# Moving the value transposes between weight pieces, and the last products with values into the scores' PSUM banks

## The chip, the cores and the metric

The kernel runs on one core of a Trainium2 chip, as one launch. The metric is the device time of the execution in microseconds. Before the change three runs gave 1260.53, 1256.4 and 1260.03 us, median 1260.03.

## What is computed

One layer of a streaming encoder, for 256 prompt frames and 64 frames of a running stream: 320 columns in all (T), held transposed, with features on the partitions. Weights and activations are float32.

```
z = rmsnorm(x) @ w_in                 # 2048 -> 1024 q | 128 k | 128 v | 1024 u | 1024 gate
q, k = rmsnorm(q), rmsnorm(k)         # per head of 64; 16 query heads, 2 kv heads
w = softmax(q k / 8 + bias, sinks)    # chunks of 64, own chunk and the two before
a = w @ v
s = gelu(u) * (W_s rmsnorm(gelu(g)) + b)
x = x + [rmsnorm(a), rmsnorm(s)] @ w_out
y = x + relu(rmsnorm(x) @ w_up)^2 @ w_down
```

Outputs are y, the new keys and values, and the normalised gate rows of the stream's frames.

## The kernel before, in words

**Products by weight pieces.** Every large product computes 256 output features for all 320 columns (`product`, `products`, L115 to L153). It goes through the contraction in pieces of four 128-row tiles. For each piece one DMA loads 128x1024 weights (`w_raw`), ScalarE rounds them to the high half `w_hi` (L108), VectorE subtracts to get the low half `w_lo` (L109), and TensorE runs 24 matmuls of 128x320 (L134): for each of four tiles and two output halves the high weights with the high and the low activations, and the low weights with the high ones. There are three slots each of `w_hi` and `w_lo`. A product with 2048 input features has four pieces, 0 to 3.

**Small work between pieces.** `between_pieces` names functions that run behind a piece: its instructions are issued after the last matmul of that piece, and the matmuls of the pieces behind it are issued after the last matmul on the list `narrow` (variable `behind`), the latest of the small TensorE instructions. When the function stands behind a product's last piece, `carry` takes that mark to the next product; otherwise it ends with the product (L141). A scheduler in the framework fills in the rest of each engine's order.

**PSUM.** `acc` has two slots of two banks for the products; `s_ps` one slot of two banks (`ps_sc`, used first for the product q0, later for attention scores); `misc` two slots of one bank each, for everything small.

**The stretch that is changed.** The products of the input projection run in this order: keys, values and q0 together, q1, q2, q3, then four for the gate (v), then four for u.

- Behind piece 2 of q2, `keys` normalises the keys, sends them and the values to the outputs, copies them to the shape that the scores need (two DMAs from GpSimd's queue, L353 and L354), and calls `values`: five TensorE transposes of 96 or 128 value columns (L326), each into a `misc` slot, each copied by VectorE to `vz` (L328).
- Behind q2, VectorE evicts its sums to `qT` (L303, `evict_q`) and ScalarE squares them (`qsq`, L308).
- Behind piece 1 of q3, `norm_q(2)` sums these squares with five small matmuls (L314, ten rows of the trace) and `attend(0)` computes the first scores (L392).
- The attention has ten units (five blocks of queries by two kv heads). `attend(i)` runs three stages: `values_of(i-3)` multiplies the turned probabilities with the values (L447) into a `misc` slot, which ScalarE copies to `ao` (L450); `scores(i)` fills `s_ps`, and VectorE, ScalarE and GpSimd make probabilities of it (L402 to L421); `turn(i-2)` transposes these (L435) in one or two parts of four transposes, each part into a `misc` slot that VectorE copies out (L437). There is one `attend` behind each of pieces 1 and 3 of q3 and the v products; `attend(10)` and `attend(11)` stand behind pieces 1 and 3 of the first u product, `attend(12)` behind piece 1 of the second. From `attend(10)` on there are no scores left. `attend(11)` is followed by `rstd_rows` (L159), whose three sums take a `misc` slot too.

Of the kernel before, what the change touches and what calls it, by code (L numbers as in the profile page):

```python
# [8 lines left out]
F32 = mybir.dt.float32  # L9
# [6 lines left out]
P = 128  # L16
# [14 lines left out]
def hymba_step_kernel(ctx: ExitStack, tc: tile.TileContext, i, o):  # L31
    nc = tc.nc
# [9 lines left out]
    ps_sc = ctx.enter_context(tc.tile_pool(name="ps_sc", bufs=1, space=bass.MemoryType.PSUM))  # L42
    ps_m = ctx.enter_context(tc.tile_pool(name="ps_m", bufs=2, space=bass.MemoryType.PSUM))

    def misc():
        return ps_m.tile([P, 512], F32, name="misc", tag="misc")
# [68 lines left out]
    def products(w, k0, nk, c0, ps, rh, rl, deep=None, between_pieces={}, halves_behind={}):  # L115

        wv = w.rearrange("(kt p) n -> p kt n", p=P)
        behind = carry.pop() if carry else None  # L120
        steps.clear()
        for a in range(0, nk, 4):
            raw = (deep or wp).tile([P, 4, 256], F32, name="w_raw", tag="w_raw")
            hi, lo = w_tiles()
            load(raw, wv[:, k0 + a:k0 + a + 4, c0:c0 + 256])
            with tc.issue_after(halves_behind[a // 4]()) if a // 4 in halves_behind else nullcontext():
                high, low = halves(raw, hi, lo)
            tail = isinstance(ps, list) and a + 4 == nk
            for k, g in [(k, g) for g in range(2) for k in range(4)] if tail else [(k, g) for k in range(4) for g in range(2)]:
                kk = a + k  # L130
                for x, (w_, r_) in enumerate(((hi, rh), (hi, rl), (lo, rh))):
                    out = ps[g][:, 0:T] if isinstance(ps, list) else ps[:, g, 0:T]
                    with tc.issue_after(behind) if behind else nullcontext():
                        mm = nc.tensor.matmul(out=out, lhsT=w_[:, k, g * P:(g + 1) * P], rhs=r_(kk),  # L134
                                              start=(kk == 0 and x == 0), stop=(kk == nk - 1 and x == 2))
            steps.append((high, low, mm.ins))
            if a // 4 in between_pieces:
                with tc.issue_after(mm.ins):
                    between_pieces[a // 4]()
                    behind = narrow[-1]  # L140
                if a + 4 == nk:  # L141
                    carry.append(behind)
# [4 lines left out]
    def acc_tile():  # L147
        return ps_acc.tile([P, 2, 512], F32, name="acc", tag="acc")

    def product(w, k0, nk, c0, rh, rl, deep=None, apart=False, **kw):  # L150
        ps = [misc(), misc()] if apart else acc_tile()
        products(w, k0, nk, c0, ps, rh, rl, deep=deep, **kw)
        return ps  # L153
# [108 lines left out]
    vz = kzv[:, 896:1664].rearrange("p (x h d) -> p x h d", x=6, h=2)  # L262
    cv = i["cv"].rearrange("k (h d) -> k h d", h=2)
# [37 lines left out]
    def evict_q(g, q_ps):  # L301
        qg = qT[:, :, 2 * g:2 * g + 2]
        nc.vector.tensor_tensor(out=qg.rearrange("p b a t -> p a b t"),  # L303
                                in0=q_ps[:, :, 0:T].rearrange("p a (b t) -> p a b t", b=5),
                                in1=rx.rearrange("p (b t) -> p b t", b=5)[:, None].to_broadcast([P, 2, 5, 64]),
                                op=ALU.mult)
        sq = sm.tile([P, 5, 2, 64], F32, name="qsq", tag="w2", bufs=4)
        nc.scalar.activation(out=sq, in_=qg, func=AF.Square)  # L308
        return sq

    def norm_q(g, sq):
        st = misc()
        for b in range(5):
            mm = nc.tensor.matmul(out=st[:, 2 * b:2 * b + 2], lhsT=sq[:, b].rearrange("p a t -> p (a t)"), rhs=hone,  # L314
                                  start=True, stop=True)
        narrow.append(mm.ins)
        r = at.tile([P, 10], F32, name="r_q", tag="r_q")
        nc.vector.tensor_scalar(out=r, in0=st[:, 0:10], scalar1=HD * EPS, scalar2=None, op0=ALU.add)
        nc.gpsimd.tensor_tensor(out=rq[:, g], in0=r, in1=nhalf[:, 0:10], op=ALU.pow)

    vn = {}

    def values():
        for x, (t0, n) in enumerate(((0, 128), (96, 96), (64, 96), (160, 96), (224, 96))):
            vps = misc()
            narrow.append(nc.tensor.transpose(out=vps[0:n, 0:P], in_=vT[:, t0:t0 + n], identity=ident).ins)  # L326
            vn[t0] = vz[:, x]
            nc.vector.tensor_copy(out=vn[t0][0:n], in_=vps[0:n, 0:P].rearrange("k (h d) -> k h d", h=2))  # L328


# [9 lines left out]
    q1_sq = []  # L340
# [6 lines left out]
    def keys():  # L347
        for dst, c in ((kn[:, 0:256], slice(0, 256)), (kn[:, 384:448], slice(256, 320))):
            nc.vector.scalar_tensor_tensor(out=dst, in0=zk[:, c], scalar=g_k, in1=rk[:, c], op0=ALU.mult, op1=ALU.mult)
        for h in range(2):  # L350
            hs = slice(h * HD, (h + 1) * HD)
            nc.vector.tensor_scalar(out=kz[hs, h], in0=kn[hs], scalar1=g_q[hs], scalar2=None, op0=ALU.mult)
        nc.gpsimd.dma_start(out=kz[HD:P, 0], in_=kz[0:HD, 0])  # L353
        nc.gpsimd.dma_start(out=kz[0:HD, 1], in_=kz[HD:P, 1])  # L354
        nc.gpsimd.dma_start(out=o["kpT"], in_=kn[:, 128:256])
        nc.gpsimd.dma_start(out=o["ksT"], in_=kn[:, 384:448])
        nc.gpsimd.dma_start(out=o["vpT"], in_=vT[:, 128:256])
        nc.gpsimd.dma_start(out=o["vsT"], in_=vT[:, 256:320])
        values()

    q2_ps = product(w_in, 0, KT, 512, xh, xl,
                    between_pieces={0: first_norms, 1: lambda: norm_q(1, q1_sq[0]), 2: keys})
    nc.gpsimd.dma_start(out=vn[224][0:32], in_=cv[96:P])
    q2_sq = evict_q(2, q2_ps)


# [74 lines left out]
    def values_of(u):  # L441
        blk_, kv = units[u]
        q0, parts = blocks[blk_][0], turned.pop(u)
        o_ps = misc()
        for x, (pt, v, n) in enumerate(parts):
            for p in range(2):
                mm = nc.tensor.matmul(out=o_ps[p * HD:(p + 1) * HD, 0:256], lhsT=v[0:n, kv],  # L447
                                      rhs=pt[0:n, p * 256:(p + 1) * 256], start=(x == 0), stop=(x == len(parts) - 1))
        narrow.append(mm.ins)
        nc.scalar.activation(out=ao[:, 4 * kv:4 * kv + 4, q0:q0 + 64],  # L450
                             in_=o_ps[:, 0:256].rearrange("p (a q) -> p a q", a=4), func=AF.Copy)

    def attend(i):

        for stage, u in ((values_of, i - 3), (scores, i), (turn, i - 2)):
            if 0 <= u < 10:
                with tc.issue_after(narrow[-1]):
                    stage(u)

    q3_ps = product(w_in, 0, KT, 768, xh, xl,  # L460
                    between_pieces={1: lambda: (norm_q(2, q2_sq), attend(0)), 3: lambda: attend(1)})
    q3_sq = evict_q(3, q3_ps)

    def add_square(acc, src, first):
# [227 lines left out]
```

## Time and profile before

| | |
|---|---|
| three runs, us | 1260.53, 1256.4, 1260.03 (median 1260.03) |
| profiled execution, us | 1259.32 |
| its span, first to last instruction, us | 1256.6 |
| mean granted TensorE clock | 0.998 |
| TensorE busy | 1246.9 us, 99% of the span |
| VectorE, ScalarE, GpSimd busy | 52%, 39%, 8% |
| memory traffic | 187.78 MB, mean 149 GB/s |

A TensorE row of the timeline gives the start, the duration of the group, line, operation and tiles, and in brackets how long the engine stood idle before it and what released it. Matmuls are pipelined, so a row of 0.31 us starts every 0.15 us. A row of the chain of waits gives start, length, engine, tile, line and count. The view by stretches gives for each engine its busy time, and behind them the granted clock, the DMA share and GB/s.

### The profile page before, as it was taken

The numbers are of one execution on the slowest core, as the hardware profiler recorded it, in microseconds if no ns is written. First come the engines' busy times: TensorE is split into PE (matmuls) and PEld (weight loads), VectorE is DVE, ScalarE is ACT, GpSimd is POOL, SyncE is SP. The second block draws the span as 40 slices with busy tenths as digits, with TensorE's granted clock in tenths as the row PEclk, the third lists the DMA queues.
The fourth block names the chain that finished last, engine by engine and source line by source line (L and its number), as shares of the span: only waits on it lengthen the run. The fifth ranks groups of instructions, "written<-read, shape, count | busy, mean of one in ns | idle before, by whom it ended". The sixth has DMA issues, their size and how long they took to land.

```text
span 1256.6 us, 20213 instructions
## 1 busy us (share of the span) xinstructions
PE 1246.9 (99%) x8519; PEld 1234.4 (98%) x8519; DVE 650.7 (52%) x767; ACT 489.6 (39%) x638; POOL 100.5 (8%) x97
## 2 busy tenths in 40 slices
PE   9999999999999999999999999999999999999998
PEld 8999989999999999999999999999999999999998
DVE  7857765776874544444444444454444334444443
ACT  7335556434543433333333322243333333343221
POOL 1114543300310000000000000000000000000000
PEclk9999999999999999999999999999999999999999
DMA  8644333644454444444454444555444454444550
GB/s 269 209 128 118 110 110 106 204 149 140 150 151 151 150 151 151 151 152 151 150 148 152 147 149 147 150 150 151 151 151 152 150 151 148 147 152 159 169 169 32
DMA packets 186556, 187.78 MB, mean 149 GB/s; under 512 B 6593, under 2 KB 185985, under 8 KB 186465
## 3 DMA queue, kind: packets, MB, share of 16 engines
q1 hardware_dynamic: 185824, 185.43, 47.6%
q8 instruction: 66, 1.08, 0.4%
q0 software_dynamic: 496, 1.03, 0.3%
q14 instruction: 26, 0.20, 0.0%
q10 hardware_dynamic: 144, 0.03, 0.0%
HBM read 182.91 MB, written 3.32 MB: 148 GB/s over the span
## 4 chain that ended last, share of the span: by engine, by line
PE 98%; ACT 1%; DVE 1%; POOL 0%; DMA 0%; issue 0%; SPq 0%; DVEq 0%; POOLq 0%
PE acc L134 91%; PE acc L240 1%; PE q_ps L240 1%; PE misc L134 1%; PE s_ps L392 1%; PE misc L435 0%; PE misc L447 0%; ACT w_hi L108 0%; PE misc L314 0%; DMA w_first<-in_w_in 0%; PE misc L521 0%; PE misc L507 0%; POOL gv L496 0%; POOL gc L479 0%; ACT s L417 0%
## 5 line engine op out<-in xcount | busy, mean ns | idle before, releaser
L109 DVE TENSOR_TENSOR w_lo<-w_raw,w_hi 128x1024 fp32r<-128x1024 f32 x332 | 413.3, 1245 | 438.4 <-ACT w_hi L108 428.7
L108 ACT ACTIVATE w_hi<-w_raw 128x1024 fp32r<-128x1024 f32 x332 | 351.7, 1060 | 705.9 <-PE acc L134 671.3
L134 PE MATMUL acc<-H2H,w_hi 128*128 128x320 f32 x1024 | 316.4, 309 | 0.0
L134 PE MATMUL acc<-H2L,w_hi 128*128 128x320 f32 x1024 | 316.4, 309 | 0.0
L134 PE MATMUL acc<-H2H,w_lo 128*128 128x320 f32 x1024 | 316.4, 309 | 0.0
L134 PE MATMUL acc<-FH,w_hi 128*128 128x320 f32 x992 | 306.5, 309 | 0.0
L134 PE MATMUL acc<-FL,w_hi 128*128 128x320 f32 x992 | 306.5, 309 | 0.0
L134 PE MATMUL acc<-FH,w_lo 128*128 128x320 f32 x992 | 306.5, 309 | 0.0
L134 PEld LDWEIGHTS acc<-H2H,w_lo 128*128 128x128 f32 x1024 | 192.2, 188 | 0.0
L134 PEld LDWEIGHTS acc<-H2H,w_hi 128*128 128x128 f32 x1024 | 192.2, 188 | 0.0
L134 PEld LDWEIGHTS acc<-H2L,w_hi 128*128 128x128 f32 x1024 | 192.2, 188 | 0.0
L134 PEld LDWEIGHTS acc<-FH,w_hi 128*128 128x128 f32 x992 | 186.2, 188 | 0.0
L134 PEld LDWEIGHTS acc<-FL,w_hi 128*128 128x128 f32 x992 | 186.2, 188 | 0.0
L134 PEld LDWEIGHTS acc<-FH,w_lo 128*128 128x128 f32 x992 | 186.2, 188 | 0.0
L134 PE MATMUL acc<-XH,w_hi 128*128 128x320 f32 x352 | 111.5, 317 | 0.0
L134 PE MATMUL acc<-XL,w_hi 128*128 128x320 f32 x352 | 109.3, 310 | 0.0
L134 PE MATMUL acc<-XH,w_lo 128*128 128x320 f32 x352 | 108.8, 310 | 0.0
L134 PEld LDWEIGHTS acc<-XH,w_hi 128*128 128x128 f32 x352 | 66.6, 189 | 0.3
L134 PEld LDWEIGHTS acc<-XL,w_hi 128*128 128x128 f32 x352 | 66.6, 189 | 0.0
L134 PEld LDWEIGHTS acc<-XH,w_lo 128*128 128x128 f32 x352 | 66.4, 189 | 0.0
L609 DVE SCALAR_TENSOR_TENSOR tf<-acc,r 128x640 f32<-128x640 f32 x32 | 26.4, 825 | 41.9 <-PE acc L134 41.8
L623 DVE TENSOR_TENSOR xT<-xT,acc 128x640 f32<-128x640 f32 x31 | 25.5, 821 | 41.8 <-PE acc L134 41.8
(201 smaller groups left out, 1056.6 us busy)
## 6 DMA issues: line engine op xcount, KB each, us to landing
w_raw<-in_w_up SPq DMA_DIRECT2D x128, 512.0 KB
w_raw<-in_w_down SPq DMA_DIRECT2D x128, 512.0 KB
w_raw<-in_w_in SPq DMA_DIRECT2D x44, 512.0 KB
w_raw<-in_w_out SPq DMA_DIRECT2D x32, 512.0 KB
w_first<-in_w_in SPq DMA_DIRECT2D x15, 256.0 KB
out_yT<-xT SPq DMA_DIRECT2D x7, 320.0 KB
xT<-in_xT SPq DMA_DIRECT2D x8, 160.0 KB
xT<-in_xT SPq DMA_DIRECT2D x4, 320.0 KB
```

Source lines behind the costliest of these rows:

```text
L108: return (pin(nc.scalar.activation(out=hi, in_=raw, func=AF.Copy)).ins, pin(nc.vector.tensor_tensor(out=lo, in0=raw, in1=hi.bitcast(F32), ...
L109: pin(nc.vector.tensor_tensor(out=lo, in0=raw, in1=hi.bitcast(F32), op=ALU.subtract)).ins)
L134: mm = nc.tensor.matmul(out=out, lhsT=w_[:, k, g * P:(g + 1) * P], rhs=r_(kk), start=(kk == 0 and x == 0), stop=(kk == nk - 1 and x == 2))
L240: mm = nc.tensor.matmul(out=ps[:, g, 0:T], lhsT=w_[:, j, k, g * P:(g + 1) * P], rhs=r_(a + k), start=(a + k == 0 and x == 0), stop=(a + k ...
L392: mm = nc.tensor.matmul(out=s_ps[:, p, j * nk:(j + 1) * nk], lhsT=qT[hs, blk_, a:a + 2].rearrange("p a t -> p (a t)"), rhs=kz[hs, kv, k0:k ...
L609: nc.vector.scalar_tensor_tensor(out=t, in0=ps[:, :, 0:T], scalar=0.0, in1=r2[:, None, :].to_broadcast([P, 2, T]), op0=ALU.max, op1=ALU.mult)
L623: nc.vector.tensor_tensor(out=xT[:, a:a + n], in0=xT[:, a:a + n], in1=p, op=ALU.add)
```

## The change

`values` takes the indices of the transposes that it is to do. The first two stay behind piece 2 of q2, the next two go behind its piece 3 (the last of the product, so that the mark is carried to q3), and the fifth goes behind piece 0 of q3, with the small DMA that fills the other rows of the same tile. `values_of` takes an `s_ps` slot for units 7, 8 and 9, and a `misc` slot for the others as before.

```diff
-    vn = {}
-
-    def values():
-        for x, (t0, n) in enumerate(((0, 128), (96, 96), (64, 96), (160, 96), (224, 96))):
+    vn = {t0: vz[:, x] for x, t0 in enumerate((0, 96, 64, 160, 224))}
+
+    def values(*xs):
+        for x in xs:
+            t0, n = ((0, 128), (96, 96), (64, 96), (160, 96), (224, 96))[x]
             vps = misc()
             narrow.append(nc.tensor.transpose(out=vps[0:n, 0:P], in_=vT[:, t0:t0 + n], identity=ident).ins)
-            vn[t0] = vz[:, x]
             nc.vector.tensor_copy(out=vn[t0][0:n], in_=vps[0:n, 0:P].rearrange("k (h d) -> k h d", h=2))
...
-        values()
+        values(0, 1)
 
     q2_ps = product(w_in, 0, KT, 512, xh, xl,
-                    between_pieces={0: first_norms, 1: lambda: norm_q(1, q1_sq[0]), 2: keys})
-    nc.gpsimd.dma_start(out=vn[224][0:32], in_=cv[96:P])
+                    between_pieces={0: first_norms, 1: lambda: norm_q(1, q1_sq[0]), 2: keys,
+                                    3: lambda: values(2, 3)})
     q2_sq = evict_q(2, q2_ps)
...
-        o_ps = misc()
+
+        o_ps = ps_sc.tile([P, 2, 512], F32, name="o_ps", tag="s_ps")[:, 0] if u > 6 else misc()
...
+    def last_values_part():
+        values(4)
+        nc.gpsimd.dma_start(out=vn[224][0:32], in_=cv[96:P])
+
     q3_ps = product(w_in, 0, KT, 768, xh, xl,
-                    between_pieces={1: lambda: (norm_q(2, q2_sq), attend(0)), 3: lambda: attend(1)})
+                    between_pieces={0: last_values_part, 1: lambda: (norm_q(2, q2_sq), attend(0)), 3: lambda: attend(1)})
```

Three places in the order of the engines' instructions show what moves. In the names, acc_636 is the sum of q2; acc_828 before, and acc_824 after, is the sum of q3.

TensorE before, just ahead of `norm_q(2)` (L314) and the first scores (L392), with the end of q2's last piece (weights 794 and 795) and of q3's piece 1 (weights 860 and 861):

```order
L134 MATMUL acc_636<-XH_117,w_hi_794 128x320
L134 MATMUL acc_636<-XL_118,w_hi_794 128x320
L134 MATMUL acc_636<-XH_117,w_lo_795 128x320
L134 MATMUL acc_828<-XH_117,w_lo_861 128x320
L134 MATMUL acc_828<-XH_117,w_hi_860 128x320
L134 MATMUL acc_828<-XL_118,w_hi_860 128x320
L134 MATMUL acc_828<-XH_117,w_lo_861 128x320
L314 MATMUL misc_889<-hone_113,qsq_825 128x2 x5
L392 MATMUL s_ps_898<-kzv_438,qT_119 128x64 x4
```

TensorE with the change, some 48 matmuls earlier in the program: the end of q2's last piece (weights 785 and 786), the third and fourth value transposes, and the start of q3:

```order
L134 MATMUL acc_636<-XH_117,w_hi_785 128x320
L134 MATMUL acc_636<-XL_118,w_hi_785 128x320
L134 MATMUL acc_636<-XH_117,w_lo_786 128x320
L327 MATMUL misc_814<-ident_88,kvx_436 96x128
L327 MATMUL misc_817<-ident_88,kvx_436 96x128
L134 MATMUL acc_824<-XH_117,w_hi_826 128x320
L134 MATMUL acc_824<-XL_118,w_hi_826 128x320
```

Before, q2's last matmul stood four matmuls ahead of `norm_q(2)`, behind 44 matmuls of q3; now all of q3's pieces 0 and 1, 48 matmuls, stand between the two.

VectorE before, from the copies of the third and fourth value transposes to `norm_q(2)`'s own step (L318), with the eviction of q2 (L303):

```order
L328 COPY kzv_438<-misc_784 96x128
L328 COPY kzv_438<-misc_787 96x128
L109 TENSOR_TENSOR w_lo_927<-w_raw_925,w_hi_926 128x1024
L328 COPY kzv_438<-misc_790 96x128
L303 TENSOR_TENSOR qT_119<-acc_636,rx_471 128x2x5x64
L109 TENSOR_TENSOR w_lo_957<-w_raw_955,w_hi_956 128x1024
L109 TENSOR_TENSOR w_lo_1020<-w_raw_1018,w_hi_1019 128x1024
L318 TENSOR_SCALAR r_q_895<-misc_889 128x10
```

VectorE with the change, the same stretch:

```order
L303 TENSOR_TENSOR qT_119<-acc_636,rx_471 128x2x5x64
L328 COPY kzv_438<-misc_814 96x128
L328 COPY kzv_438<-misc_817 96x128
L109 TENSOR_TENSOR w_lo_927<-w_raw_925,w_hi_926 128x1024
L328 COPY kzv_438<-misc_855 96x128
L109 TENSOR_TENSOR w_lo_957<-w_raw_955,w_hi_956 128x1024
L318 TENSOR_SCALAR r_q_895<-misc_889 128x10
L109 TENSOR_TENSOR w_lo_1020<-w_raw_1018,w_hi_1019 128x1024
```

The eviction of q2 moved ahead of three copies and a weight piece, and one weight piece moved behind L318.

ScalarE before, from the rounding of q3's piece 1 (w_hi_860) to the squares of q2:

```order
L108 ACTIVATE w_hi_860<-w_raw_859 128x1024
L108 ACTIVATE w_hi_926<-w_raw_925 128x1024
L108 ACTIVATE w_hi_956<-w_raw_955 128x1024
L108 ACTIVATE w_hi_1019<-w_raw_1018 128x1024
L308 ACTIVATE qsq_825<-qT_119 128x640
```

ScalarE with the change:

```order
L108 ACTIVATE w_hi_860<-w_raw_859 128x1024
L108 ACTIVATE w_hi_926<-w_raw_925 128x1024
L308 ACTIVATE qsq_821<-qT_119 128x640
L108 ACTIVATE w_hi_956<-w_raw_955 128x1024
L108 ACTIVATE w_hi_1019<-w_raw_1018 128x1024
```

The squares of q2 moved ahead of the rounding of two weight pieces (the last of q3 and the first of the v products).

In the last three units TensorE's instructions keep their places; the products with values (L447, now L448) write `o_ps` instead of `misc`. On VectorE the second copy of `turn(8)` (L437, to vnat) now stands ahead of a weight piece's L109 that it followed.

## The prediction

> **What bounds the kernel now.** I read the page first, then TensorE's own list of waits, then the chain of waits and the timelines around the two long ones.
>
> The page, span and busy time of the engines:
>
> ```profile
> span 1256.6 us, 20213 instructions
> PE 1246.9 (99%) x8519; PEld 1234.4 (98%) x8519; DVE 650.7 (52%) x767; ACT 489.6 (39%) x638; POOL 100.5 (8%) x97
> ```
>
> TensorE, busy for 99% of the span, sets the time; the change takes no matmul away. It can only win back what TensorE waits or runs slowly, and every microsecond won there moves the end by one. The list of what TensorE's matmuls waited for (total, times, longest):
>
> ```profile
> PE misc L435 <- DVE kzv L437: 2.1, 1, 2.1
> PE misc L314 <- ACT qsq L308: 2.0, 1, 2.0
> PE misc L435 <- ACT ao L450: 0.4, 1, 0.4
> PE misc L159 <- DVE kzv L437: 0.3, 1, 0.3
> ```
>
> All four stand in stretches that the change touches: the second in `norm_q(2)`, the others in `attend(10)`, `attend(11)` and the sums behind it. The chain of waits around the second:
>
> ```profile
> 70.70 3.54 PE acc L134 x24
> 74.26 0.84 DVE qT L303
> 75.10 1.02 ACT w_hi L108
> 76.12 0.64 ACT qsq L308
> 76.80 1.28 PE misc L314 x10
> 78.07 1.03 PE s_ps L392 x8
> 79.10 8.33 PE acc L134 x48
> ...
> 88.07 7.23 PE acc L134 x48
> 95.31 1.01 PE misc L314 x10
> ...
> 124.57 0.59 PE s_ps L392 x8
> ```
>
> TensorE finishes q2 only at 74.2, VectorE then evicts it (L303), ScalarE squares it behind other work, and `norm_q(2)` stands until 76.8. The same work also runs slower than its like elsewhere: 1.28 against 1.01, 1.03 against 0.59 (scores of the same 64 columns), 8.33 against 7.23 for 48 matmuls. The view by stretches shows why, in the column behind POOL, the granted clock:
>
> ```profile
> 78.00:81.50 3.50, 3.50 (x18) 3.38 (x18) 1.84 (x9) 0.61 (x4) 1.98 (x1) 0.51 0.87 280
> ```
>
> In the 3.5 us behind the wait the clock is 0.51.
>
> **The transposes: eviction of q2 comes early.** ScalarE, TensorE and VectorE there:
>
> ```profile
> 67.55 1.06 ACT L108 ACTIVATE w_hi<-w_raw 128x1024 fp32r<-128x1024 f32 x1 [2.90 <-PE acc L134]
> 74.11 2.00 ACT L108 ACTIVATE w_hi<-w_raw 128x1024 fp32r<-128x1024 f32 x2 [5.50 <-PE acc L134]
> 76.02 0.72 ACT L308 ACTIVATE qsq<-qT 128x640 f32<-128x640 f32 x1
> ...
> 76.80 1.28 PE L314 MATMUL misc<-hone,qsq 128*128 128x2 f32 x10 [1.99 <-ACT qsq L308]
> ...
> 63.85 0.49 DVE L328 COPY kzv<-misc 128x128 f32<-128x128 f32 x2 [0.43 <-PE misc L326]
> 65.98 0.93 DVE L352 TENSOR_SCALAR kzv<-kvx,cols 64x448 f32<-64x448 f32 x2
> 74.26 0.82 DVE L303 TENSOR_TENSOR qT<-acc,rx 128x640 f32<-128x640 f32 x1 [3.23 <-PE acc L134]
> ```
>
> All five transposes stand behind piece 2 of q2 and borrow two slots, so the scheduler spread them over the next matmuls; q2's own last piece must follow the fifth, and q3's first 44 matmuls went ahead of it. With the change q2's last piece follows the second transpose directly. The order says so for all three engines. Piece by piece at the trace's pace (24 matmuls 3.54 us): q2 ends about 67.5, where the trace had the end of q3's piece 0; VectorE is free from 66.9 (L352) and evicts 67.6 to 68.4; ScalarE, done with one weight piece at 68.6, squares until 69.3. `norm_q(2)` is reached at about 74.8, where the idle time began (76.80 - 1.99). That leaves 5.5 us of cover, so I take the wait as gone:
>
> - the wait itself: 1.99
> - `norm_q(2)`: 1.28 - 1.01 = 0.27
> - scores: 1.03 - 0.59 = 0.44
> - the 48 matmuls: 8.33 - 7.23 = 1.10
>
> Sum 3.80, of which 1.81 is the slow clock and 1.99 the wait. Without the wait the small work is 1.01 + 0.59 = 1.60 us. Behind piece 1 of the first v product it is longer, 2.37 us with `norm_q(3)`, wider scores and transposes, and the clock stays at 1.00:
>
> ```profile
> 95.14:97.51 2.37, 2.37 (x24) 2.13 (x23) 1.16 (x2) 1.06 (x1) 1.78 (x2) 1.00 0.76 220
> ```
>
> [...]
>
> **What could be late next there.** Transposes three and four now stand ahead of all of q3, at 67.5; their slots must be free, which needs VectorE's first two copies (done 64.34): cover 3.1 us. The fifth at about 71.2 needs a slot from a copy that now stands behind the eviction, about 68.7: cover 2.5. If a cover went, TensorE would stand, since the order has nothing else there. VectorE's weight piece that moved behind L318 (w_lo_1020) is done about 77.1 and needed by the first v product, some 48 matmuls (7.2 us) behind the scores: cover 6. Scores now start at about 75.8 instead of 78.07, and need the two key copies:
>
> ```profile
> 67.26 0.52 POOL L354 DMA_DIRECT2D kzv<-kzv  x1
> kzv<-kzv POOLq DMA_DIRECT2D x2, 112.0 KB, 4.4
> ```
>
> Issued by 67.8 and landed 4.4 later, 72.2: cover 3.6. The cv DMA (L363, now L463) keeps its place in GpSimd's queue, waits for the fifth copy as before, and its rows are read first by `values_of(4)`, in `attend(7)`. I count these at nothing; less than nothing is excluded, since none is waited for now.
>
> **The last three units.** TensorE's rows of the unbroken turn at 162.83 and of `attend(10)`, VectorE's of `attend(11)`, and ScalarE's copy in `attend(10)`:
>
> ```profile
> 162.83 1.08 PE L435 MATMUL misc<-ident,s 128*96 128x128 f32 x8
> 171.89 0.64 PE L435 MATMUL misc<-ident,s 128*96 128x128 f32 x4
> 174.67 0.64 PE L435 MATMUL misc<-ident,s 128*96 128x128 f32 x4 [2.14 <-DVE kzv L437]
> ...
> 183.33 1.22 DVE L109 TENSOR_TENSOR w_lo<-w_raw,w_hi 128x1024 fp32r<-128x1024 f32 x1
> 184.47 0.68 DVE L437 COPY kzv<-misc 96x512 f32<-96x512 f32 x1
> ...
> 174.28 0.36 ACT L450 ACTIVATE ao<-misc 128x256 f32<-128x256 f32 x1
> ```
>
> In `attend(10)` three things want two slots: `values_of(7)`, and the two parts of `turn(8)`. The second part waits 2.14 us for VectorE's copy of the first; ScalarE's copy of the values ends with it at 174.64. With the values in `s_ps`, both parts have a slot at once. Saved: the wait 2.14, and 0.64 + 0.64 - 1.08 = 0.20 of the broken row: 2.34. No dip follows this wait, as 47 matmuls then take 6.91 us, so none is won:
>
> ```profile
> 175.31 6.91 PE acc L134 x47
> ```
>
> `s_ps` is free there: its last reader is VectorE's step on unit 9's scores, which come right ahead of the row of 162.83. It is one slot, so `values_of(8)`, due 2.3 us sooner at about 180, waits for ScalarE's copy of unit 7, done 174.64: cover 5.3.
>
> In `attend(11)` the 0.4 behind ScalarE's copy goes, but the sums (L159, 0.3 in the list) still wait for VectorE's copy of the first part (184.47), which stands behind a weight piece (183.33) that follows TensorE's own pace. I count nothing; at most 0.4 + 0.3 = 0.7. In `attend(12)` I also count nothing.
>
> **Sum.** 3.80 + 2.34 = 6.14 us. The profiled execution took 1259.32, 2.7 of it outside its span of 1256.6 and untouched: 1259.32 - 6.14 = 1253.2. It lies 0.7 below the median of the three runs, inside their spread of 4.1.
>
> **The rivals.**
>
> *A, the dip stays.* The wait goes, and the clock dips all the same, as the small work of 1.60 us is still there. Price 1.81: 1253.2 + 1.8 = 1255.0. For it: a wait as long, 2.14 us, at 174 is followed by no dip, so length alone does not make one. Against it: 2.37 us of small work at 95.14 make none either. [...]
>
> *B, the wait of `attend(10)` moves on.* The second part of `turn(8)` no longer waits, but VectorE's copies stay where they are (that of the first part ended just ahead of 174.67), and something else stands for them. Price 2.34: 1255.5. Against it: no small work that needs a slot follows for two pieces of 3.5 us.
>
> *C, q2's end is early and `norm_q(2)` still waits,* for the scores' keys or a slot, or the order does not hold on the chip: only the second place gains, 1259.32 - 2.34 = 1257.0. Against it: the covers of 3.6 and 5.5.
>
> *D, slower.* The transposes become a gate. Three and four hold all of q3, the fifth holds its piece 1, and TensorE stands for VectorE's copies, with nothing queued that may pass. It decides from a lateness of 3.1 us beyond the trace's pace at the first, 2.5 at the second. To turn the sum, the two waits with a dip of 1.81 each must exceed 6.14, so 2.5 us of waiting in all; to be slower by more than 0.3% (3.8 us) 6.3, or 3.15 each: 1253.2 + 6.3 + 3.6 = 1263.1, with the 0.7 to the median 1263.8. Against it: VectorE, 52% busy over the span, sat idle for 3.23 us ahead of 74.26.
>
> **How the numbers follow.** Forecast 0.66, A 0.11, B 0.10, C 0.06, D 0.03, no change at all 0.04. The likeliest is the forecast, 1253.2. Down, the range takes in the 0.7 of `attend(11)` and the 2.9 by which the fastest of the three runs lies below the profiled one, most of it: 1250.0. Up, it takes in A and B and the 0.7 to the median, 1256.2, and most of C: 1256.6. About 0.3% of the time, 3.8 us, is what a measurement can tell from no change. Faster by more, below 1256.25: forecast, nearly all of A and B: 0.81. Within: C, no change, and the rest: 0.15. Slower: 0.04.
>
> **What would show it.** In the profile of the changed kernel: the eviction of q2 (L303) at about 67.6 and its squares below 70; `norm_q(2)` at about 74.7 with no idle time ahead of it, and the granted clock at 1.00 between 74 and 82 (A if not); the next scores' 48 matmuls in 7.2 us; `turn(8)` in one row of eight at about 168; the last matmul some 6 us earlier in the span. It would be wrong if TensorE's list of waits names L327, L392 or L448 with more than 1 us, or if a wait of 2 us stands at L159.

## The result

| | before | after |
|---|---|---|
| median, us (five runs of each) | 1260.53 | 1251.18 |
| lowest to highest, us | 1256.4 to 1263.5 | 1251.05 to 1252.61 |
| profiled execution, us | 1259.32 | 1251.18 |
| its span, us | 1256.6 | 1249.4 |
| mean granted TensorE clock | 0.998 | 1.000 |

The ratio of after to before is 0.993, 95% interval 0.9908 to 0.9952: faster by 9.35 us at the median, where 6.14 was forecast against the profiled execution. The time lies in the range and 2.0 below the number. One of the twelve executions of e9 below ran at a mean clock of 0.203 and took 5707.55 us; it is left out of e9's row.

The busy times on the page and TensorE's list of waits after the change:

```profile
PE 1243.7 (100%) x8519; PEld 1231.9 (99%) x8519; DVE 650.8 (52%) x767; ACT 489.4 (39%) x638; POOL 102.1 (8%) x97
```

```profile
PE misc L78 <- DVE hone L91: 1.3, 1, 1.3
PE misc L159 <- DVE kzv L437: 0.8, 1, 0.8
```

The wait for the squares (L314) and both waits at L435 are gone. L78 is at the program's start, before as after; L159 has 0.8 where 0.4 (L435) and 0.3 (L159) stood at two places. The chain of waits after, at both places:

```profile
62.79 0.22 PE misc L327 x2
...
73.90 1.01 PE misc L314 x10
74.91 0.59 PE s_ps L392 x8
75.50 7.23 PE acc L134 x48
82.73 0.65 PE s_ps L392 x8
...
167.26 1.01 PE misc L435 x8
168.27 6.90 PE acc L134 x47
...
178.16 0.83 PE misc L159 x6
...
188.02 1.00 PE misc L512 x8
```

All the small work runs at its undisturbed length, and nothing stands between 62.79 and 82.73 but TensorE's own work. The timeline (VectorE's eviction of q2, ScalarE's squares) and the view by stretches, in which the 1.00 behind POOL is the granted clock:

```profile
66.56 0.82 DVE L303 TENSOR_TENSOR qT<-acc,rx 128x640 f32<-128x640 f32 x1 [0.57 <-PE acc L134]
67.42 0.74 ACT L308 ACTIVATE qsq<-qT 128x640 f32<-128x640 f32 x1
```

```profile
78.00:81.50 3.50, 3.50 (x26) 3.50 (x25) 1.36 (x4) 2.48 (x10) 0.83 (x2) 1.00 0.41 139
```

The squares end at 68.16, 5.7 us ahead of their reader at 73.90.

### The profile page after: what moved, and what is told of

Read it like the earlier page. It is cut to its first block, busy times and chain, and to the rows that moved or that the text cites. A ratio compares the mean times of both kernels' runs of the same rounds, so it can differ in the third digit from the quotient of the medians.

```text
span 1249.4 us, 20216 instructions
## 1 busy us (share of the span) xinstructions
PE 1243.7 (100%) x8519; PEld 1231.9 (99%) x8519; DVE 650.8 (52%) x767; ACT 489.4 (39%) x638; POOL 102.1 (8%) x97
## 3 DMA queue, kind: packets, MB, share of 16 engines
q0 software_dynamic: 496, 1.03, 0.3%
## 4 chain that ended last, share of the span: by engine, by line
PE 97%; DMA 2%; SPq 1%; ACT 0%; DVE 0%; issue 0%; ACTq 0%; DVEq 0%
PE acc L134 91%; PE misc L134 1%; DMA w_raw<-in_w_in 1%; SPq L103 1%; PE misc L435 1%; PE s_ps L392 1%; DMA b_dram<-b_row 1%; PE q_ps L240 0%; PE acc L240 0%; PE misc L448 0%; PE misc L314 0%; PE misc L526 0%; PE misc L512 0%; DMA cols<-in_cols 0%; ACT w_hi L108 0%
## 5 line engine op out<-in xcount | busy, mean ns | idle before, releaser
L109 DVE TENSOR_TENSOR w_lo<-w_raw,w_hi 128x1024 fp32r<-128x1024 f32 x332 | 413.7, 1246 | 434.6 <-ACT w_hi L108 425.1
L134 PE MATMUL acc<-H2H,w_hi 128*128 128x320 f32 x1024 | 316.4, 309 | 0.0
L134 PE MATMUL acc<-H2L,w_hi 128*128 128x320 f32 x1024 | 316.4, 309 | 0.0
L134 PE MATMUL acc<-H2H,w_lo 128*128 128x320 f32 x1024 | 316.4, 309 | 0.0
L134 PE MATMUL acc<-FH,w_hi 128*128 128x320 f32 x992 | 306.5, 309 | 0.0
L134 PE MATMUL acc<-FL,w_hi 128*128 128x320 f32 x992 | 306.5, 309 | 0.0
L134 PE MATMUL acc<-FH,w_lo 128*128 128x320 f32 x992 | 306.5, 309 | 0.0
L134 PEld LDWEIGHTS acc<-H2L,w_hi 128*128 128x128 f32 x1024 | 192.3, 188 | 0.0
L134 PEld LDWEIGHTS acc<-H2H,w_hi 128*128 128x128 f32 x1024 | 192.3, 188 | 0.0
L134 PEld LDWEIGHTS acc<-H2H,w_lo 128*128 128x128 f32 x1024 | 192.3, 188 | 0.0
L134 PEld LDWEIGHTS acc<-FH,w_hi 128*128 128x128 f32 x992 | 186.2, 188 | 0.0
L134 PEld LDWEIGHTS acc<-FL,w_hi 128*128 128x128 f32 x992 | 186.2, 188 | 0.0
L134 PEld LDWEIGHTS acc<-FH,w_lo 128*128 128x128 f32 x992 | 186.2, 188 | 0.0
L134 PE MATMUL acc<-XH,w_hi 128*128 128x320 f32 x352 | 111.1, 316 | 0.1
L134 PE MATMUL acc<-XL,w_hi 128*128 128x320 f32 x352 | 108.7, 309 | 0.0
L134 PE MATMUL acc<-XH,w_lo 128*128 128x320 f32 x352 | 108.6, 309 | 0.0
L134 PEld LDWEIGHTS acc<-XH,w_hi 128*128 128x128 f32 x352 | 66.2, 188 | 0.6 <-ACT ksq L338 0.4
L134 PEld LDWEIGHTS acc<-XL,w_hi 128*128 128x128 f32 x352 | 66.2, 188 | 0.0
L134 PEld LDWEIGHTS acc<-XH,w_lo 128*128 128x128 f32 x352 | 66.0, 188 | 0.0
```

The lines of the kernel that those rows point to most:

```text
L109: pin(nc.vector.tensor_tensor(out=lo, in0=raw, in1=hi.bitcast(F32), op=ALU.subtract)).ins)
```

## The experiments

The theory after the result had two parts: each half of the change removes one wait of about 2 us, and a wait can bring a slow stretch of the clock behind it whose cost differs from execution to execution. The rival: the gain beyond 6.1 was luck of single executions, or the slow stretch has another cause than the wait. All medians below stand beside runs of the kernel before on the same chip (medians 1260.5 to 1261.5; e1, e2, e3 and e7 stand beside 1261.5, all others beside 1260.5 to 1260.7). The last column is the mean granted clock, averaged over the runs of the row. With about half of a stretch at half clock taken as lost (1.54 of 3.41 us in e2 below), a mean clock that is 0.001 lower stands, as an estimate, for 1.26 us lost of a span of 1259 us; what is said below of slow clock in medians is this estimate. The runs of before beside them have 0.9961 to 0.9967.

| kernel | median, us (lowest to highest, runs) | ratio to before, 95% | clock |
|---|---|---|---|
| e0, after again | 1251.30 (1250.83 to 1252.79, 5) | 0.9926 [0.9912, 0.9940] | 0.9998 |
| e1, after without the `s_ps` slots | 1256.21 (1255.45 to 1258.21, 6) | 0.9957 [0.9942, 0.9971] | 0.9987 |
| e2, before with the `s_ps` slots | 1256.90 (1256.11 to 1258.68, 6) | 0.9961 [0.9946, 0.9975] | 0.9983 |
| e3, after, squares late | 1256.80 (1253.74 to 1258.19, 6) | 0.9957 [0.9941, 0.9973] | 0.9988 |
| e5, before, squares earlier | 1258.61 (1256.95 to 1262.46, 12) | 0.9985 [0.9975, 0.9996] | 0.9978 |
| e6, after, sums in `s_ps` too | 1250.61 (1250.17 to 1251.59, 4) | 0.9919 [0.9904, 0.9934] | 1.0000 |
| e7, after, squares later still | 1260.23 (1259.09 to 1264.36, 12) | 0.9996 [0.9984, 1.0008] | 0.9962 |
| e8, before, norm_q(2) later | 1254.61 (1253.91 to 1259.17, 9) | 0.9958 [0.9944, 0.9971] | 0.9990 |
| e9, before, wait filled | 1258.25 (1256.52 to 1262.54, 11) | 0.9984 [0.9971, 0.9997] | 0.9988 |
| e11, after, more small work | 1256.03 (1254.31 to 1259.86, 12) | 0.9966 [0.9954, 0.9978] | 0.9985 |

e4 and e10 were one execution each, and their times stand with them.

**Is the gain that large (e0)?** The changed kernel unaltered.

> The changed kernel itself, beside runs of the kernel before on the same chip. By the theory (two waits of 2.0 and 2.1 us gone, and with them whatever slow clock they bring), 1251 to 1253 us again with a mean clock of 1.00 in each run, and 8 to 10 us below the median of before. If the 8.1 us between the two profiled executions were mostly luck of the one execution (0.9 at the start and 0.9 outside the span), about 6.

It is: 1251.30, 9.4 below before. Its profiled span was 1250.2; the 9 us are no luck. The clocks say how much of it is slow clock: 0.9998 against 0.9967 in the 23 runs of before beside it is 3.9 us of a span of 1259.

**Each half alone (e1, e2).**

```diff
# e1, on the changed kernel
-        o_ps = ps_sc.tile([P, 2, 512], F32, name="o_ps", tag="s_ps")[:, 0] if u > 6 else misc()
+        o_ps = misc()
# e2, on the kernel before: the reverse
```

> The change with the products with values back in misc slots. Theory (two separate terms): the wait of norm_q(2) and the slow clock behind it go, 3.8 us of 1260.5, so about 1256.7; TensorE's list keeps about 2.1 us at L435 and has nothing at L314; the 48 matmuls behind the first scores take 7.2 us. Rival (the two places share the misc slots, so one alone brings little): less than 1.5 us is won. Rival (most of the gain is the second place): about 1258.

> The kernel before with only units 7, 8 and 9 in the scores' banks. Theory: turn(8) is one row of eight, 2.3 us are won, about 1258.2; norm_q(2) still waits 2.0 us, and the granted clock of the runs is below 1.00 in those whose dip comes. [...]

e1 gained 5.3 us, e2 4.6: together 9.9, about what both give. The chain of e1, in which L435 waits as before:

```profile
77.17 1.01 PE misc L314 x10
...
78.78 7.23 PE acc L134 x48
...
173.90 6.90 PE acc L134 x47
```

And that of e2:

```profile
77.05 1.28 PE misc L314 x10
...
78.91 8.77 PE acc L134 x48
```

Each half mends its own place only: the first place is clean in e1 (1.01 and 7.23) and still slow in e2, where the slow stretch came later, past the scores (from 80.12), and cost 8.77 - 7.23 = 1.54. The row of `norm_q(2)` has its 1.28 there ahead of the slow stretch: the 0.27 above 1.01 belongs to the wait and not to the clock. The second half was worth more than its 2.34 of wait and broken row: 4.6. The mean clock gives most of the rest: 0.9983 in e2 against 0.9961 is 2.8 us, and e10 shows where it lay in one execution.

**The kernel before once more (e10).** Unaltered, one execution.

> The kernel before once more, for a second profile of it. Its executions on this chip have a mean clock of 0.994 to 0.998. Theory: both waits, 2.0 us near 75 and 2.1 us near 172, can bring a slow stretch, now one and now both, and a run with 0.995 or 0.996 shows a dip behind each, or one of two windows of 3.4 us. Rival: the slow stretches lie elsewhere, away from both waits.

1264.65 us, mean clock 0.994: slower than all 13 runs of before beside it (1257.09 to 1262.95), so a slow example and not a typical one. TensorE's waits and the chain of this execution:

```profile
PE acc L134 <- ACT ksq L338: 2.5, 1, 2.5
PE misc L435 <- DVE kzv L437: 2.1, 1, 2.1
PE misc L314 <- ACT qsq L308: 2.0, 1, 2.0
```

```profile
51.81 5.29 PE acc L134 x24
...
79.75 1.53 PE misc L314 x10
81.28 1.05 PE s_ps L392 x8
82.34 9.56 PE acc L134 x48
...
179.78 8.43 PE acc L134 x47
```

The same two waits, 2.1 and 2.0, but the clock took more: 0.25 (1.53 less 1.28) + 0.46 + 2.33 = 3.0 at the first place and 8.43 - 6.90 = 1.5 at the second, where the execution of the prediction lost nothing. Together 4.6, against 1.54 in the execution of the prediction. A third place is ahead of the change, 2.5 us of waiting near 50 us and 5.29 for 24 matmuls; the wait is in kernels with and without the change (0.5 to 2.5 in most profiles, none in some), a slow stretch follows it in two profiles of fourteen (e10 without the change, e1 with its first half), and it is no part of the change. The view by stretches, cut at the edges of the slow stretches:

```profile
77.19:80.60 3.41, 1.42 (x12) 1.16 (x11) 3.18 (x3) 2.51 (x3) 0.00 (x0) 1.00 0.03 3
80.60:84.01 3.41, 3.41 (x18) 3.28 (x19) 1.69 (x9) 0.00 (x0) 1.98 (x1) 0.50 0.93 290
84.01:87.42 3.41, 3.41 (x14) 3.41 (x14) 0.49 (x4) 1.53 (x9) 0.61 (x1) 0.50 0.06 21
...
176.17:179.58 3.41, 1.28 (x13) 0.86 (x9) 2.14 (x5) 3.27 (x11) 2.54 (x4) 1.00 0.47 147
179.58:182.99 3.41, 3.41 (x15) 3.41 (x14) 1.28 (x2) 0.00 (x0) 2.00 (x1) 0.50 0.41 111
```

The clock is 1.00 or 0.50 in these stretches. Finer stretches put the two falls at 80.62 and 179.61, 98.99 us apart, and the rises behind them at 87.45 and 183.02: 6.83 and 3.41 us at half clock. In the 3.41 us ahead of the falls TensorE (first pair behind the length) worked 1.42 and 1.28.

**Does the wait bring the slow clock? Fill it (e9).**

```diff
     def norm_q(g, sq):
         st = misc()
+        for _ in range(13 if g == 2 else 0):
+            nc.tensor.matmul(out=st[:, 0:T], lhsT=xh(0)[:, 0:P], rhs=xh(0), start=True, stop=True)
```

> The kernel before, with 13 matmuls of 128x320 (1.96 us at 0.15 each) put ahead of norm_q(2), into the slot that it then overwrites: TensorE works where it waited, and nothing else is changed. Theory (the idle time brings the slow clock): no dip behind it, norm_q 1.01, scores 0.59, 48 matmuls 7.23, and 1.8 us per execution with one dip below before, up to 3.5 where before has two. Rival (the small matmuls, or chance, bring it): the dip stays and the time is that of before.

```profile
76.94 1.28 PE misc L316 x10
...
78.81 7.24 PE acc L134 x48
...
174.35 7.83 PE acc L134 x47
```

The end of q2 is as late as before, `norm_q(2)` begins at the same point, and no slow stretch follows: 7.24. Its row takes 1.28, as in before, at full clock. (The untouched second wait brought a slow stretch here, from 172.87: 7.83.) The gain, 2.0 us by the ratio (0.4 to 3.7), is clock alone: the filling takes up the wait, and the mean clock rose from 0.9967 to 0.9988, 2.6 us.

**Is it the transposes' place, or only the squares' lateness (e8)?**

```diff
-                    between_pieces={1: lambda: (norm_q(2, q2_sq), attend(0)), 3: lambda: attend(1)})
+                    between_pieces={2: lambda: (norm_q(2, q2_sq), attend(0)), 3: lambda: attend(1)})
```

> The kernel before, with norm_q(2) and attend(0) one piece of q3 later (3.5 us), the transposes left where they were. Theory (all that the transposes' move wins is that q2's squares are done in time): the wait of 2.0 goes with its dip, 3.8 us below before in an execution with one dip there. Rival: attend(1) now follows 3.5 us behind attend(0), and its scores wait for the one s_ps slot; then a wait stands at L392 and the gain is smaller by it.

```profile
78.33 1.01 PE misc L314 x10
79.34 0.59 PE s_ps L392 x8
79.93 3.71 PE acc L134 x24
```

The wait went without moving a transpose, and no wait came at L392. The gain, 5.3 us by the ratio (3.7 to 7.1), is that of e1 (5.4): where the transposes stand is worth nothing in itself that these runs could tell.

**How much waiting is enough (e5, e3, e7)?** e5 puts ScalarE's squares one weight piece sooner in the kernel before; e3 and e7 make them late in the changed one, by a scale of 1.0 that TensorE must deliver first, e7 with three more squares ahead.

```diff
# e5 (squares[-1] is the activation that squares q2)
...
+                    halves_behind={3: lambda: squares[-1]})
# e3; e7 issues three more such activations ahead of the last
+    def late_squares():
+        one_ps = misc()
+        narrow.append(nc.tensor.matmul(out=one_ps[:, 0:2], lhsT=ident, rhs=ones_c, start=True, stop=True).ins)
...
+        nc.scalar.activation(out=sq, in_=qT[:, :, 4:6], func=AF.Square, scale=one[:, 0:1])
+        norm_q(2, sq)
...
```

> The kernel before, with ScalarE's squares of q2 ahead of the rounding of one weight piece instead of behind it: TensorE's wait ahead of norm_q(2) falls from 2.0 to about 1.0 us, the transposes stay. If the dip needs only some idle time, it stays: 1.0 below before. If it needs most of 2 us, it goes as well: 2.8 or more below before, and no stretch of 3.4 us with a clock near 0.5 behind it in the profile.

> The change, but the squares of q2 are made late on purpose: ScalarE takes a scale of 1.0 for them that TensorE makes behind piece 1 of q3 (one small matmul and one copy more). norm_q(2) should stand some 1.5 us again with all transposes where the change puts them. Theory (late squares are the whole cause, the places of the transposes as such are worth nothing): 1.5 us are lost against the change, and up to 1.8 more in runs in which the clock dips: 1252.7 to 1254.5. Rival (the order of transposes itself brings the gain): no more than the 0.3 of the added matmul, 1251.5.

> As the one before, with three more squares of 0.64 us each on ScalarE ahead of the one that counts: a wait of some 3.5 us. [...] Rival (length of the wait does not matter for the dip, the small work behind it does): the change had the same small work and no dip, so 3.5 and no dip, 1254.7.

The waits, and for e5 and e3 the chain behind; e5, whose profiled execution is the slowest of its twelve runs:

```profile
PE misc L316 <- ACT qsq L310: 1.1, 1, 1.1
```

```profile
77.08 1.52 PE misc L316 x10
78.60 1.05 PE s_ps L394 x8
79.65 9.56 PE acc L134 x48
```

e3, whose profiled execution is the fastest of its six runs:

```profile
PE misc L318 <- ACT qsq L475: 1.6, 1, 1.6
```

```profile
76.18 1.28 PE misc L318 x10
...
78.05 7.23 PE acc L136 x48
```

e7:

```profile
PE misc L318 <- ACT qsq L477: 4.2, 1, 4.2
```

A wait of 1.1 was followed by a slow stretch of 6.83 us (the clock is 0.50 from 77.95 to 84.78), one of 1.6 by none, one of 4.2 by 10.24 us (76.54 to 86.78). In these three the length of the wait alone doesn't decide. Halving it (e5) won 1.9 us by the ratio (0.5 to 3.2) and left the slow clock in place in the profiled execution. e3 puts a wait back into the changed kernel and costs about 4 us by the ratios (0.9957 against 0.9926), more than its profiled execution lost, and its mean clock of 0.9988 says that other runs had a slow stretch. e7 costs nearly 9, of which 4.2 is the wait and most of the rest, as an estimate, the 10.24 us of slow work behind it. Both cost more than was expected of them.

**Is it idle time, or small work (e11)?** The changed kernel with the ten rows of `norm_q(2)` done three times, and no wait.

```diff
-        for b in range(5):
+        for b in [b for _ in range(3 if g == 2 else 1) for b in range(5)]:
```

> The changed kernel, with the matmuls of norm_q(2) done three times over into the same slot (128x2, 30 rows of the trace instead of 10): 2.0 us more of small work (1.01 per ten), and no wait. [...]

The chain, and the stretches cut at the slow one:

```profile
74.89 3.24 PE misc L314 x30
...
78.73 8.76 PE acc L134 x48
```

```profile
76.28:79.69 3.41, 3.41 (x32) 3.33 (x32) 1.92 (x7) 0.00 (x0) 1.19 (x1) 1.00 0.45 129
79.69:83.10 3.41, 3.41 (x15) 3.41 (x14) 1.13 (x6) 1.53 (x9) 1.26 (x2) 0.50 0.18 63
```

TensorE is busy for 3.41 of 3.41 us, and the clock is 0.50 in the 3.41 us behind them. If only idle time brought the slow clock, it would have stayed at 1.00 here, with 7.23 instead of 8.76 for the 48 matmuls and a time 2.2 above the changed kernel. So that answer fell, and with it the theory in the form that e9 was run under. Of those 3.41 us only 1.03 are wide matmuls (L134); 1.85 are the 128x2 matmuls of L314 (to 78.13) and 0.59 the scores. Ten of the twelve runs have a mean clock below 1.000, against one of the ten runs of the changed kernel (result and e0). The median is 4.7 us above e0; 2.23 of it is the added work itself.

**The last three units apart (e4, e6).** e4 keeps only unit 7 in `s_ps`; e6 moves the sums at L159 there too.

```diff
# e4
-... if u > 6 else misc()
+... if u == 7 else misc()
# e6
-            rv.append(rstd_rows(acc_v, inv_1k, 4 * EPS))
+            rv.append(rstd_rows(acc_v, inv_1k, 4 * EPS, ps_sc.tile([P, 2, 512], F32, name="st_v", tag="s_ps")[:, 0]))
```

> The changed kernel, with only unit 7's product with values in the scores' bank, units 8 and 9 in misc slots as before. Theory: only attend(10) had a wait that the bank removes, so the wait of attend(11) is the same 0.8 in all, split between L435 (0.4 behind ScalarE's copy) and L159, and the span is that of the changed kernel within 0.2 us. Rival (attend(11) and attend(12) gained too): 0.4 to 0.7 us longer at attend(11).

> The changed kernel, with the three sums behind attend(11) in the scores' bank too. Theory: the wait of 0.83 at L159 is for a misc slot (VectorE's copy of the first part of the turn), so it goes, and the time is 0.8 us below the changed kernel beside it. Rival: the wait moves to the next that takes a misc slot, the products behind the sums or attend(12), and the time stays within 0.2.

e4 took 1252.43 us. Its span, 1250.7, is 1.3 above that of the result and not within the 0.2 expected, but 1.09 of this was there at the unbroken turn already (168.35 against 167.26). The chain of e4:

```profile
168.35 1.01 PE misc L435 x8
...
189.12 1.14 PE misc L512 x8
```

And of e6:

```profile
167.68 1.01 PE misc L435 x8
...
177.74 0.76 PE st_v L159 x6
...
187.54 1.00 PE misc L512 x8
```

From the unbroken turn to the row at L512 are 20.77 us in e4, 20.76 after, 19.86 in e6. So units 8 and 9 in `s_ps` win nothing in `attend(11)`, and 0.14 in `attend(12)` (1.14 to 1.00); in e6 the last wait went, 0.9 with the shorter row (0.76 for 0.83). Its median is 0.7 below e0, but the runs of the two overlap, so that the timing alone doesn't separate them. By the trace it is the best version tried.

## Why the prediction was right, and where it was not

Taken at starts of rows in the two chains, before minus after. The execution after was ahead by 0.91 already at the first transposes (63.70 against 62.79), which is no work of the change.

- **Transposes, 3.80.** Measured 3.79: the scores of `attend(1)` start at 82.73 instead of 87.43 (79.10 + 8.33), 4.70 less the 0.91. All four pieces came out as priced, and the eviction at 66.56 and `norm_q(2)` at 73.90 are the 67.6 and 74.7 of the forecast less those 0.9, to within 0.2. One reading was wrong without moving the sum: the 0.27 of `norm_q(2)` is not slow clock. Its row ended at 78.08, where the clock fell at 78.06, and it takes 1.28 at full clock in e9 and e3 too, wherever the squares come just in time or late. So the slow clock's part was 0.44 + 1.10 = 1.54 and the wait's 1.99 + 0.27 = 2.26.
- **The covers** of transposes, weight piece, scores and keys held: no wait names L327 or L392. Rivals C and D, and the one that the change does nothing, fall.
- **Rival A** fell: the clock is 1.00 from 74 to 81.5. Its reason was nearer the truth than the forecast's, though: 3.83 us of small work with no wait were followed by half clock in e11. The 1.60 that is left here was not.
- **`attend(10)`, 2.34.** Measured 2.34: 175.31 against 168.27 is 7.04, less the 4.70. Rival B fell.
- **`attend(11)`, 0.** Right, and e4 shows why: the wait for VectorE's copy gathers at L159 as 0.83, where before and in e4 0.37 stand at L435 and 0.26 at L159; the 0.20 between is what the unbroken row of the turn saves.
- **`attend(12)`, 0.** It won 0.14.
- **Sum.** 3.79 + 2.34 + 0.14 = 6.27 against 6.14. The profiled executions differ by 8.14: the rest is the 0.91 ahead of the change and 0.94 outside the spans (2.72 and 1.78), both "untouched" in the forecast and lucky here.
- **The step that failed** is "No dip follows this wait, as 47 matmuls then take 6.91 us, so none is won". That was true of one execution. Of six profiles with that wait (before, e1, e5, e8, e9, e10) two show 6.9 and four 7.83 to 8.43 for the 47 matmuls. The first place's 1.54 was at the low end likewise, with 3.0 in e10 and e5. The slow clock's term, 1.54 in the sum, is 9.35 - (6.27 - 1.54) = 4.6 in the medians. The clocks on record agree: the 69 runs of before that stand beside the experiments have 0.9965 on average, 4.4 us of their span, and the ten of the changed kernel 0.9999, 0.1 us; the profiled execution of the prediction had 0.998, half as much. With it gone the spread of the runs fell as well, from 7.1 to 1.6 us.
- **The range** held, in part by luck: it reached down to 1250.0 for the 0.7 of `attend(11)`, which did not come, and for the fastest of three runs, and not for a slow clock behind the second wait.

That the median of before carried more slow clock than the profiled execution showed in its spread of 4.1 us, which I took for noise to be covered and not for the clock. The profile had it too, from 78.06 to 81.47. Why none followed the wait of `attend(10)` there (172.53 to 174.67) is not shown; an estimate can be made from e10, where the falls at 80.62 and 179.61 lie 98.99 us apart, 29 times 3.413, where one slow stretch measures 3.41. Counted on in this profile, 28 such lengths from 78.06 end at 173.63, in the middle of that wait:

```profile
170.22:173.63 3.41, 2.31 (x17) 1.33 (x16) 2.14 (x5) 2.88 (x12) 3.41 (x4) 1.00 0.53 154
173.63:177.05 3.42, 2.38 (x17) 2.38 (x18) 2.78 (x5) 1.37 (x3) 2.54 (x2) 1.00 0.05 8
```

Divided there, the wait is shared by two stretches, each with over 2.3 us of work, and no slow stretch followed (6.91 for the 47 matmuls). In e10 the stretch shown from 176.17 held all of the wait, with 1.28 us of work beside it, and the clock fell behind it.

## What to carry to other kernels

Here, with TensorE busy for 99% of the span, each of two waits of about 2 us between dense stretches cost its length and, in some executions, 0.9 (7.83 less 6.90 in e9) to 3.0 us (e10) of half clock behind it; price such a wait by more than one profile, or by the spread and the mean clocks of the runs. Both edits that closed the gap at `norm_q(2)` won both, the one that moved the producer sooner (e1, 5.4 us by the ratio) and the one that moved the consumer later (e8, 5.3); filling the gap with 13 wide matmuls (e9, 2.0 us) won the clock alone, and 3.24 us of narrow ones with no gap (e11) were followed by half clock. A wait of 2.1 us on a PSUM slot was bought off with a bank that had gone idle, but only the use that was waited for gained (2.34 for unit 7, 0.14 for units 8 and 9).

## What the runs showed of the clock

In the finest stretches read of these profiles (0.1 us) the granted clock is 1.00 or 0.50, but for the few in which it changes. It did not fall at one place of the program: in the first profile of before at 78.06, at the end of `norm_q(2)`'s row (78.08), in the second (e10) at 80.62, in the middle of that row (79.75 to 81.28). Slow stretches lasted 3.41 us (78.06 to 81.47 in before), 6.83 (80.62 to 87.45 in e10) and 10.24 (76.54 to 86.78 in e7). Two falls of one profile lay 98.99 us apart in e10 (80.62 and 179.61) and in e5 (77.95 and 176.94).

The 3.41 us ahead of a fall had 0.58 (e10, from 77.19), 1.03 (e11, from 76.28) and 1.39 us (e5, from 74.59) of wide matmuls (L134) in them, with TensorE busy for 1.42, 3.41 and 2.31. But stretches of the same length with 0.74 (e1, from 181.81) and 1.35 us (e10, from 189.83) of L134 and TensorE busy for 2.78 were followed by a clock of 1.00, so neither number alone parts the two kinds. A close pair are two stretches with 1.65 us of work in e9 and 1.72 in e1:

```profile
169.49:172.90 3.41, 1.65 (x13) 0.87 (x12) 2.14 (x5) 3.19 (x12) 3.10 (x4) 1.00 0.50 156
171.57:174.98 3.41, 1.72 (x13) 1.73 (x14) 3.23 (x5) 2.01 (x5) 2.53 (x3) 1.00 0.16 54
```

The first was followed by half clock (from 172.87), the second was not. Behind a slow stretch with 1.74 us of L134 (e10, from 80.60) a second slow one followed, behind one with 2.48 (before, from 78.10) none.

e3 had a wait of 1.6, longer than e5's 1.1, and its clock is 1.00 in every stretch of 0.1 us between 46 and 90 us. What decides is not shown by these profiles.
